# Cross-covariance attention on one core: Q and K of four units in rows of 8 KB

## The chip, the cores and the metric

The kernel runs on one core of a Trainium2 chip. The metric is the device time in microseconds. The kernel before takes 127.44 us, the median of three runs (127.34 to 127.64).

## The reference

For each of 8 x 12 = 96 heads, Q, K and V are 512 x 64 in f32. Q and K are normalised along the sequence, so each of the 64 columns is divided by its own norm; the attention is 64 x 64, column against column:

```python
Q_norm = Q / (np.linalg.norm(Q, axis=-2, keepdims=True) + 1e-10)
K_norm = K / (np.linalg.norm(K, axis=-2, keepdims=True) + 1e-10)
attn = np.einsum('bhnd,bhne->bhde', Q_norm, K_norm)
attn = np.exp(attn - np.max(attn, axis=-1, keepdims=True))
attn = attn / (np.sum(attn, axis=-1, keepdims=True) + 1e-10)
return np.einsum('bhnd,bhde->bhne', V, attn).astype(np.float32)
```

Three inputs of 12.6 MB are read once and one output of 12.6 MB is written.

## The kernel before

The 96 heads are 12 units (s) of 8 heads. Two units make a pair (w), and V is loaded by pairs, in two halves of 1 MB.

Loads. `load_qk` (L213 to L223) brings Q or K of one unit, 1 MB, into a tile of 128 partitions. A head has 32 partitions and each of them 16 consecutive sequence rows, which are 4 KB in a row in memory; the 8 heads of a unit are two groups (r) of four, so a partition holds two such rows, one for each group. Unit 0 comes in halves (FINE). `load_v` (L225) gives a V head 16 partitions with 32 sequence rows each, 8 KB in a row. There are 7 buffers for Q and K together (`NB['qk']`), 3 for V and 6 for outputs (`NB['so']`).

Work on a unit. `cast_qk` (L244) makes bf16 copies with the two groups interleaved. `square` (L249) squares them for the norms, Q and K into one tile. `grams` (L258 to L263) runs 64 matmuls: for each of 16 sequence rows and each head slot h, the 32 partitions of a slot, 128 columns of K (two heads) against 128 of Q; of the 128 x 128 result only the two 64 x 64 diagonal blocks are used. `sums` (L265) adds the squares over partitions with a 0/1 matrix (`hm`), `fold` (L272) adds up the rest on DVE, `norms` (L276) turns the sums over with a selecting matrix, `powers` (L280) takes the power -1/2 on ACT. `scale_k` (L286) multiplies the gram by K's norms, `logits` (L290) transposes it on PE, `scales_q` (L294) multiplies by Q's norms in two halves, `exps` and `normalise` (L300, L304) make the attention matrix `ab` in bf16.

Work on V and the output. `cast_v` (L316), `vtrans` (L321, transposes on PE), `vcopy` (L328), then `outs` (L334, 32 matmuls for a quarter of a unit), `ocopy` (L344, out of PSUM into an output tile) and `store` (L229), 1 MB for a unit. The store of unit 9 is cut into four (CUTS, one of them 124 partitions and one 4), and units 10 and 11 are stored in halves (HALF).

The order. All DMAs but two are issued by SP, in one queue. A planner (`Order`, L75) writes out one order for all engines before anything is built: each piece of work has engines with a cost, pieces that must be done first, and a rank (R, and QK_PACE, V_FROM, V_PACE, ST_LAG for DMAs); where several pieces can start at about the same time, the lowest rank goes first. A piece that may run on several engines (CHOICE) is put where cost plus BIAS ends first. Casts may be on DVE, ACT or POOL, squares on DVE or ACT, `vcopy` and `ocopy` on ACT or DVE. A DMA of 512 KB is costed at X = 1.27 us, and at most 8 are in flight. Each engine then runs its list in that order.

Of the kernel before, what the change touches and what calls it, by code (L numbers as in the profile page):

```python
# [18 lines left out]
 'R': {'ck': 14.3601,  # L19
       'q': -46.9145,  # L20
       'sq': -4.5261,
       'sk': 21.309,
       'gr': 31.9137,
       's1': -8.269,
       'rd': 14.1273,
       'nn': -13.565,
       'pw': -22.1669,
       'kx': 16.8281,
       'lg': -36.3133,
       'qs': 14.727,  # L30
       'ex': 7.4539,
       'nm': 23.5766,
       'cv': -5.1919,
       'vt': 13.5707,
       'vc': 31.4911,
       'ou': -17.6156,
       'oc': 6.4318},
 'BIAS': {('cv', 'DVE'): 12.3272,
          ('vc', 'ACT'): 5.2627,
          ('oc', 'DVE'): 7.9654,  # L40
          ('q0', 'ACT'): -9.0842,
          ('sk', 'ACT'): 4.174,
          ('sk', 'DVE'): 5.4091,
          ('cv', 'ACT'): 0.906,
          ('cv', 'POOL'): -0.1651,
          ('ck', 'DVE'): -11.8527,
          ('ck', 'ACT'): -10.4645,
          ('ck', 'POOL'): -15.4937,
          ('oc', 'ACT'): 4.7795,
          ('sq', 'DVE'): -12.3114,  # L50
          ('sq', 'ACT'): -21.9953,
          ('q0', 'DVE'): -28.6804,
          ('q0', 'POOL'): -29.3142,
          ('vc', 'DVE'): -20.4676},
 'QK_PACE': 0.9356,
 'V_FROM': 0.0874,
 'V_PACE': 0.7666,
 'ST_LAG': 6.0835,
 'SPLIT': 3,
 'HALF': (10, 11),  # L60
 'WAKE': ('SP',),
 'CUTS': ((0, 0, 6, 0, 124), (0, 0, 6, 124, 128), (0, 6, 16, 0, 128), (1, 0, 16, 0, 128))}
# [89 lines left out]
def kernel(  # L152
# [13 lines left out]
    FINE = PAR["FINE"]  # L166
# [13 lines left out]
    qmp = ctx.enter_context(tc.tile_pool(name="qmp", bufs=NB["qm"]))  # L180
    sqp = ctx.enter_context(tc.tile_pool(name="sqp", bufs=NB["sq"]))
# [59 lines left out]
    def heads(c):  # L241
        return slice(0, 2) if c is None else slice(c, c + 1)

    def cast_qk(eng, s, x, c):  # L244
        if (s, x) not in qkb:
            qkb[s, x] = qmp.tile([128, TT, 2, D], BF16, name="qb" if x == 0 else "kb")
        copy(eng, qkb[s, x][:, :, heads(c)], qk32[s, x][:, cols(c)].rearrange("p (r t) d -> p t r d", t=TT))

    def square(eng, s, x, c):  # L249
        if s not in sq:  # L250
            sq[s] = sqp.tile([128, 2, TT, 2, D], BF16, name="sq")
        o, i = sq[s][:, x, :, heads(c)], qkb[s, x][:, :, heads(c)]
        if eng == "ACT":
            nc.scalar.activation(o, i, AF.Square)  # L254
        else:
            nc.vector.tensor_tensor(out=o, in0=i, in1=i, op=ALU.mult)

    def grams(s):  # L258
        gram[s] = ps_g.tile([128, HU, 4, 2 * D], F32, name="gram")
        for t in range(TT):  # L260
            for h in range(HU):
                q, k = (qkb[s, x][32 * h:32 * (h + 1), t].rearrange("p r d -> p (r d)") for x in range(2))
                nc.tensor.matmul(gram[s][:, h, 0], k, q, start=(t == 0), stop=(t == TT - 1))  # L263

    def sums(s):  # L265
        st[s] = ps_l.tile([D, 4, 2 * D], F32, name="l")
        for t in range(0, TT, 4):
            for x in range(2):
                nc.tensor.matmul(st[s][32 * x:32 * (x + 1)].rearrange("p t d -> p (t d)"), hm,  # L269
                                 sq[s][:, x, t:t + 4].rearrange("p t r d -> p (t r d)"), start=(t == 0), stop=(t == TT - 4))  # L270

    def fold(s):  # L272
        s2[s] = small.tile([D, 2 * D], F32, name="s2")
        nc.vector.tensor_reduce(out=s2[s], in_=st[s].rearrange("p t d -> p d t"), axis=mybir.AxisListType.X, op=ALU.add)  # L274

    def norms(s):  # L276
        nn[s] = ps_l.tile([128, 2 * HU], F32, name="l")
        nc.tensor.matmul(nn[s], s2[s], sel, start=True, stop=True)  # L278

    def powers(s):  # L280
        ln = small.tile([128, 2 * HU], F32, name="ln")
        r12[s] = small.tile([128, 2 * HU], F32, name="r12")
# [3 lines left out]
    def scale_k(s):  # L286
        kqs[s] = small.tile([128, HU, 2 * D], F32, name="kqs")
        nc.vector.tensor_tensor(out=kqs[s], in0=gram[s][:, :, 0], in1=r12[s][:, HU:, None].to_broadcast([128, HU, 2 * D]), op=ALU.mult)  # L288

    def logits(s):  # L290
        for h in range(HU):
            nc.tensor.transpose(gram[s][:, h, 1], kqs[s][:, h], ident)  # L292

    def scales_q(s, r):  # L294
        if r == 0:
            ls[s] = small.tile([128, HU, D], F32, name="ls")
        half = (LO, HI)[r]
        nc.vector.tensor_tensor(out=ls[s][half], in0=gram[s][half, :, 1, half], in1=r12[s][half, :HU, None].to_broadcast([D, HU, D]), op=ALU.mult)  # L298
# [66 lines left out]
    hm = const.tile([128, 32], BF16, name="hm")  # L365
    nc.gpsimd.memset(hm, 0.0)
    own = const.tile([128, HU], F32, name="own")
    nc.vector.tensor_reduce(out=own, in_=ident.rearrange("p (h i) -> p h i", h=HU), axis=mybir.AxisListType.X, op=ALU.add)
    nc.vector.tensor_copy(hm[:, 0:HU], own)
    sel = const.tile([D, 2 * HU], F32, name="sel")  # L370
    for x in range(2):
        nc.gpsimd.tensor_copy(sel[:, HU * x:HU * (x + 1)], ident[0:D, 32 * x:32 * x + HU])
# [6 lines left out]
    def size(key):  # L379
        n = {"gr": 128, "s1": 16, "nn": 4, "lg": 8, "vt": 8, "ou": 32}[key[0]]  # L380
        return n // 2 if key[0] == "vt" and key[-1] is not None else n

    LOCK = {"ck", "q0", "sq", "sk", "nm", "cv"}
# [11 lines left out]
    CHOICE = ("ck", "q0", "sq", "sk", "cv", "vc", "oc")  # L395
# [17 lines left out]
    def uses(i):  # L413
        s, x = divmod(i, 2)
        return every("ck" if x else "q0", s)

    last = None
    for s in range(S):
        for c in parts(s):
            for x in range(2):  # L420
                key = ("l" + "qk"[x], s, c)
                piece(key, {"DMA": 2 * X if c is None else X}, uses(2 * s + x - NB["qk"]), [last],
                      PAR["QK_PACE"] * ((s + 0.5 * (c or 0)) / S), load_qk, s, x, c)
                last = key
    SM = NB["sm"]
    for s in range(S):
        for c in parts(s):
            dve, act, tt = two(c, 0.16, 0.52), two(c, 0.18, 0.84), two(c, 0.16, 0.52)
            for x, (load, cast, sqr, rank) in enumerate((("lq", "q0", "sq", "q"), ("lk", "ck", "sk", "ck"))):
                free = [("gr", s - NB["qm"])] + every(sqr, s - NB["qm"]) if s >= NB["qm"] else []  # L430
                piece((cast, s, c), {"DVE": dve, "ACT": act, "POOL": 2 * dve}, [(load, s, c)] + free, [], R[rank] + 0.01 * s, cast_qk, s, x, c)
                piece((sqr, s, c), {"DVE": tt, "ACT": act}, [(cast, s, c), back("s1", s, NB["sq"])], [], R[sqr] + 0.01 * s, square, s, x, c)
        piece(("gr", s), {"PE": 1.2}, every("ck", s) + every("q0", s) + [back("qs", s, 1, 0), back("qs", s, 1, 1)], [], R["gr"] + 0.01 * s, grams, s)
        piece(("s1", s), {"PE": 1.2}, every("sk", s) + every("sq", s) + [back("pw", s, 1)], [], R["s1"] + 0.01 * s, sums, s)
        piece(("rd", s), {"DVE": 0.69}, [("s1", s), back("nn", s, SM)], [], R["rd"] + 0.01 * s, fold, s)
        piece(("nn", s), {"PE": 0.3}, [("rd", s)], [], R["nn"] + 0.01 * s, norms, s)
        piece(("pw", s), {"ACT": 0.52}, [("nn", s), back("qs", s, SM, 0), back("qs", s, SM, 1)], [], R["pw"] + 0.01 * s, powers, s)
        piece(("kx", s), {"DVE": 0.69}, [("gr", s), ("pw", s), back("lg", s, SM)], [], R["kx"] + 0.01 * s, scale_k, s)
        piece(("lg", s), {"PE": 0.7}, [("kx", s)], [], R["lg"] + 0.01 * s, logits, s)
        for r in range(2):  # L440
            piece(("qs", s, r), {"DVE": 0.43}, [("lg", s), back("ex", s, SM)], [("qs", s, 0)] if r else [], R["qs"] + 0.01 * s, scales_q, s, r)
        piece(("ex", s), {"ACT": 0.425}, [("qs", s, 0), ("qs", s, 1), back("nm", s, SM)], [], R["ex"] + 0.01 * s, exps, s)
# [6 lines left out]
    for w in range(W):  # L449
# [9 lines left out]
        for n, (q, f) in enumerate(turns(w)):  # L459
# [3 lines left out]
            else:  # L463
                wait = [("qs", S - 1, 0), ("qs", S - 1, 1)] + ([("vc", w, *turns(w)[n - 4])] if n >= 4 and turns(w)[n - 4][1] is not None else [])
# [57 lines left out]
```

## Time and profile before

| what | value |
|---|---|
| median of 3 runs | 127.44 us (127.34 to 127.64) |
| the profiled execution | 127.3 us |
| its span, first to last instruction | 125.2 us |
| TensorE clock granted, mean | 0.875 |
| HBM read, written | 37.75 MB, 12.58 MB |
| instructions | 4066 |

The profile is of one execution. Its first part gives the busy time of each engine, its second cuts the span in 40 slices and shows the busy share of each in tenths, its third the DMA queues; q1 is SP's queue, q10 ACT's, q8 and q14 are instruction fetches and small loads. The chain follows the work that ended last back to the start. Groups of instructions are named by line and tiles; times of one instruction are in ns. The sixth part gives DMA issues by tile, with their size and the median time from issue to landing. PE is TensorE, DVE VectorE, ACT ScalarE, POOL GpSimd, SP SyncE.

### The profile page before, as it was taken

Reading aid. Unit: us, or ns where it says so; the run is one execution under the profiler, and the core shown is the slowest. Engines: PE = TensorE matmul, PEld = TensorE weight load, DVE = VectorE, ACT = ScalarE, POOL = GpSimd, SP = SyncE. Lnnn points to the kernel's source line nnn. Section 1 sums busy time; section 2 is a strip of 40 time slices with the busy share of each in tenths; the row PEclk is TensorE's granted clock in tenths of the full one; section 3 lists DMA queues with packets and bytes.
Section 4 is the critical chain, followed back from the end, with each engine's and each line's share of the span. In section 5 each row is a group of like instructions: output and inputs, shape, how many; then the busy total and the mean of one; then the engine's idle time right before and its main releaser. Section 6 shows DMA issues by size and latency. Waiting matters only on the chain.

```text
span 125.2 us, 4066 instructions
## 1 busy us (share of the span) xinstructions
PE 79.2 (63%) x1800; PEld 52.6 (42%) x1800; DVE 78.9 (63%) x140; ACT 84.9 (68%) x116; POOL 47.5 (38%) x40
## 2 busy tenths in 40 slices
PE   0019369873598787859637798882898879941000
PEld 0024254561474475538525455461275456630000
DVE  2043475876852989987987599993799978700000
ACT  4068594784698853998799997938958697863000
POOL 3330665382627088061806925065144810000000
PEclk9999955999657999995999999999599999997555
DMA  3999999999999999999999999999999999999993
GB/s 129 399 419 431 424 411 418 427 419 415 420 424 423 420 428 408 421 414 428 410 432 424 410 421 415 429 414 420 427 428 410 416 416 414 418 408 412 415 395 154
DMA packets 11785, 50.59 MB, mean 404 GB/s; under 512 B 888, under 2 KB 1016, under 8 KB 10232
## 3 DMA queue, kind: packets, MB, share of 16 engines
q1 hardware_dynamic: 11480, 49.29, 95.8%
q10 hardware_dynamic: 288, 1.05, 2.3%
q8 instruction: 14, 0.23, 0.7%
q14 instruction: 3, 0.02, 0.0%
HBM read 37.75 MB, written 12.58 MB: 402 GB/s over the span
## 4 chain that ended last, share of the span: by engine, by line
DMA 70%; PE 9%; ACT 5%; DVE 4%; issue 2%; SPq 1%; ACTq 0%
DMA qk<-in_Q_dram 37%; DMA out_dram<-so 17%; DMA qk<-in_K_dram 16%; ACT so L207 5%; PE po L341 3%; PE gram L263 2%; PE gram L292 1%; PE vps L326 1%; DVE kqs L288 1%; DVE qb L209 1%; PE l L269 1%; DVE ab L313 1%; DVE s L274 0%; PE l L278 0%; ACT ln L283 0%
## 5 line engine op out<-in xcount | busy, mean ns | idle before, releaser
L211 POOL TENSOR_SCALAR kb<-qk 128x2048 bf16<-128x2048 f32 (+1 forms) x13 | 23.0, 1771 | 37.8 <-DMA qk<-in_K_dram 30.9
L254 ACT ACTIVATE sq<-qb 128x2048 bf16<-128x2048 bf16 (+1 forms) x13 | 23.1, 1776 | 7.8 <-DVE qb L209 7.6
L207 ACT COPY so<-po 128x512 f32<-128x512 f32 x47 | 25.6, 584 | 3.9 <-PE po L341 2.3
L211 POOL TENSOR_SCALAR vb<-v 128x1024 bf16<-128x1024 f32 x15 | 21.4, 1444 | 13.4 <-DMA v<-in_V_dram 9.6
L341 PE MATMUL po<-ab,vt 128*32 128x128 bf16 x768 | 20.2, 232 | 6.6 <-ACT so L207 2.1
L263 PE MATMUL gram<-qb,kb 32*128 32x128 bf16 x768 | 15.5, 237 | 12.3 <-DVE qb L209 8.8
L209 DVE CAST qb<-qk 128x2048 bf16<-128x2048 f32 (+1 forms) x12 | 13.7, 1143 | 11.2 <-DMA qk<-in_Q_dram 10.7
L326 PE MATMUL vps<-ident,vb 128*128 128x128 f32 x96 | 17.3, 305 | 4.7 <-POOL vb L211 2.7
L269 PE MATMUL l<-sq,hm 128*32 128x512 bf16 x96 | 18.4, 442 | 1.7 <-ACT sq L254 1.6
L263 PEld LDWEIGHTS <-kb 32*128 32x128 bf16 x768 | 13.3, 104 | 14.4 <-POOL kb L211 10.3
L341 PEld LDWEIGHTS <-vt 128*32 128x32 bf16 x768 | 13.8, 101 | 12.4 <-issue 7.9
L209 DVE COPY vt<-vps 128x1024 bf16<-128x1024 bf16 (+1 forms) x25 | 16.5, 665 | 3.4 <-PE vps L326 3.1
L207 ACT CAST vb<-v 128x1024 bf16<-128x1024 f32 x9 | 12.1, 1341 | 8.8 <-DMA v<-in_V_dram 8.6
L254 ACT ACTIVATE sq<-kb 128x2048 bf16<-128x2048 bf16 (+1 forms) x10 | 17.3, 1733 | 0.6 <-POOL kb L211 0.6
L326 PEld LDWEIGHTS vps<-ident,vb 128*128 128x128 f32 x96 | 11.2, 151 | 8.5 <-POOL vb L211 3.2
L274 DVE TENSOR_REDUCE s<-l 64x128 f32<-64x512 f32 x12 | 8.1, 677 | 6.5 <-PE l L269 6.5
L298 DVE TENSOR_TENSOR ls<-gram,r 64x256 f32<-64x256 f32 x24 | 10.1, 420 | 2.2 <-PE gram L292 1.9
L292 PE MATMUL gram<-ident,kqs 128*128 128x128 f32 x48 | 9.0, 316 | 3.5 <-DVE kqs L288 3.0
L288 DVE TENSOR_TENSOR kqs<-gram,r 128x512 f32<-128x512 f32 x12 | 8.3, 689 | 3.7 <-ACT r L284 3.1
L313 DVE TENSOR_TENSOR ab<-ex,rb 128x512 bf16<-128x512 f32 x12 | 9.3, 773 | 0.4
L269 PEld LDWEIGHTS <-hm 128*32 128x32 bf16 x96 | 5.5, 104 | 9.4 <-issue 7.4
L292 PEld LDWEIGHTS gram<-ident,kqs 128*128 128x128 f32 x48 | 5.7, 154 | 7.4 <-DVE kqs L288 6.6
(25 smaller groups left out, 40.2 us busy)
## 6 DMA issues: line engine op xcount, KB each, us to landing
v<-in_V_dram SPq DMA_DIRECT2D x12, 1024.0 KB, 19.8
qk<-in_Q_dram SPq DMA_DIRECT2D x11, 1024.0 KB, 19.8
qk<-in_K_dram SPq DMA_DIRECT2D x11, 1024.0 KB, 19.6
out_dram<-so SPq DMA_DIRECT2D x9, 1024.0 KB, 19.7
out_dram<-so SPq DMA_DIRECT2D x5, 512.0 KB, 9.4
qk<-in_K_dram ACTq DMA_DIRECT2D x2, 512.0 KB, 4.6
qk<-in_Q_dram SPq DMA_DIRECT2D x2, 512.0 KB, 6.3
out_dram<-so SPq DMA_DIRECT2D x1, 320.0 KB, 10.1
```

The costliest lines, as they stand in the source:

```text
L207: nc.scalar.copy(o, i)
L209: nc.vector.tensor_copy(o, i)
L211: nc.gpsimd.tensor_scalar(out=o, in0=i, scalar1=1.0, scalar2=0.0, op0=ALU.mult, op1=ALU.add)
L254: nc.scalar.activation(o, i, AF.Square)
L263: nc.tensor.matmul(gram[s][:, h, 0], k, q, start=(t == 0), stop=(t == TT - 1))
L269: nc.tensor.matmul(st[s][32 * x:32 * (x + 1)].rearrange("p t d -> p (t d)"), hm, sq[s][:, x, t:t + 4].rearrange("p t r d -> p (t r d)"), s ...
L288: nc.vector.tensor_tensor(out=kqs[s], in0=gram[s][:, :, 0], in1=r12[s][:, HU:, None].to_broadcast([128, HU, 2 * D]), op=ALU.mult)
L292: nc.tensor.transpose(gram[s][:, h, 1], kqs[s][:, h], ident)
L298: nc.vector.tensor_tensor(out=ls[s][half], in0=gram[s][half, :, 1, half], in1=r12[s][half, :HU, None].to_broadcast([D, HU, D]), op=ALU.mult)
L313: nc.vector.tensor_tensor(out=ab[s], in0=ex[s][:, :, None, :].to_broadcast([128, HU, 2, D]), in1=rb[:, :, :, None].to_broadcast([128, HU, ...
L326: nc.tensor.transpose(ps[:, n], vb[w][:, j].rearrange("p r d c -> p (r d c)").bitcast(F32), ident)
L341: nc.tensor.matmul(po[s, x][32 * h:32 * (h + 1), j].rearrange("p r d -> p (r d)"), v, ab[s][:, h].rearrange("p r d -> p (r d)"), start=Tru ...
```

## The change

Q and K of units 1 to 4 (LONG) are loaded like V: a head has 16 partitions with 32 sequence rows each, 8 KB in a row. The two groups of heads then lie in the two halves of the partitions, and each half is a DMA of its own, of 64 partitions. Such a unit is worked on differently:

- 32 partitions, one slot of the matmuls, now hold two heads. Q is copied twice to bf16 (`mask_q`), once with the partitions of the odd head set to zero and once with those of the even one (`par` is a 0/1 column); K is copied once, without interleaving.
- The gram matmul takes K (128 columns: two sequence rows) against both masked copies of Q (256 columns).
- Q is squared from its f32 tile, on ACT only.
- The two sequence rows are added up after the gram: `logits` multiplies by `eye2`, two identities one above the other, in place of the transpose. `scale_k` runs in two halves, `scales_q` in one step.
- The norms have other selecting matrices (`hm`, `sel` with 12 columns), built at the start by a few more small instructions.

For all units the squares of Q and K have a tile each, and their sums are separate pieces, each with two row groups of PSUM (b = 32 * (2 * x + n % 2)). The ranks and biases of the planner are all new, so the order of all work and the engine of most casts and copies differ. POOL's cost for casts in the planner is 1.5 times DVE's in place of 2. Buffers keep their numbers; the bf16 copies of K get a pool of their own.

```diff
+ 'LONG': (1, 2, 3, 4),
+ 'XL': 1.2575,
...
+    Ql, Kl = (x.rearrange("b h (p t) d -> (b h p) (t d)", t=T).rearrange("(w r e p) x -> w e r p x", r=2, e=2, p=4 * T // 2) for x in (Q, K))
...
-        if c is None:
+        if s in LONG:
+            for r, half in enumerate((LO, HI)):
+                issue.dma_start(out=o[half], in_=(Ql, Kl)[x][w, e, r])
+        elif c is None:
...
+        if s in LONG:
+            qkb[s, x] = kbp.tile([128, T, D], BF16, name="kb")
+            copy(eng, qkb[s, x], qk32[s, x])
+            return
...
+    def mask_q(eng, s, r):
+        if (s, 0) not in qkb:
+            qkb[s, 0] = qmp.tile([128, 2, T, D], BF16, name="qb")
+        o, i, m = qkb[s, 0][:, r], qk32[s, 0], par[:, r:r + 1]
+        if eng == "ACT":
+            nc.scalar.activation(o, i, AF.Copy, scale=m)
+        else:
+            (nc.vector if eng == "DVE" else nc.gpsimd).tensor_scalar(out=o, in0=i, scalar1=m, scalar2=0.0, op0=ALU.mult, op1=ALU.add)
...
+                p = slice(32 * h, 32 * (h + 1))
+                if s in LONG:
+                    o = gram[s][:, h, 0:2]
+                    q, k = qkb[s, 0][p, :, 2 * t:2 * t + 2].rearrange("p r t d -> p r (t d)"), qkb[s, 1][p, 2 * t:2 * t + 2].rearrange("p t d -> p (t d)")
...
+            if s in LONG:
+                nc.tensor.matmul(gram[s][:, h, 2, LO], kqs[s][:, h], eye2, start=True, stop=True)
+            else:
+                nc.tensor.transpose(gram[s][:, h, 1], kqs[s][:, h], ident)
...
- 'QK_PACE': 0.9356,
- 'V_FROM': 0.0874,
- 'V_PACE': 0.7666,
- 'ST_LAG': 6.0835,
+ 'QK_PACE': 15.9432,
+ 'V_FROM': 1.2527,
+ 'V_PACE': 10.4878,
+ 'ST_LAG': 17.0031,
```

On SP's queue the loads now come in the order V, Q1, K1, V, Q2, K2, V and so on, where before Q1, K1, V, V, Q2, K2 began it. Two full stores are issued before the last V load, where one was.

More of the change, by code (lines that the diff above doesn't have):

```diff
@@ L18 @@
  'X': 1.27,
[L19 to L54, printed above, removed]
@@ L55 @@
- 'QK_PACE': 0.9356,
- 'V_FROM': 0.0874,
- 'V_PACE': 0.7666,
- 'ST_LAG': 6.0835,
+ 'R': {'ck': -22.4355,
+       'q': -58.979,
+       'sq': 8.8953,
+       'sk': 87.461,
+       'gr': 115.1078,
+       's1': 72.6482,
+       'rd': 61.2414,
+       'nn': -14.167,
+       'pw': -122.7448,
+       'kx': -4.8738,
+       'lg': -47.4763,
+       'qs': -27.9749,
+       'ex': 38.4008,
+       'nm': -4.3242,
+       'cv': -20.2888,
+       'vt': 86.5781,
+       'vc': -27.908,
+       'ou': 26.3559,
+       'oc': 86.0175},
@@ new lines @@
+ 'BIAS': {('cv', 'DVE'): 3.5472,
+          ('vc', 'ACT'): 33.8237,
+          ('oc', 'DVE'): 9.7574,
+          ('q0', 'ACT'): 8.6126,
+          ('sk', 'ACT'): -50.3485,
+          ('sk', 'DVE'): 76.2585,
+          ('cv', 'ACT'): 2.2132,
+          ('cv', 'POOL'): 3.0663,
+          ('ck', 'DVE'): 28.4022,
+          ('ck', 'ACT'): -2.9809,
+          ('ck', 'POOL'): -27.8906,
+          ('oc', 'ACT'): 9.3321,
+          ('sq', 'DVE'): 33.0171,
+          ('sq', 'ACT'): 32.675,
+          ('q0', 'DVE'): -43.3867,
+          ('q0', 'POOL'): -44.9347,
+          ('vc', 'DVE'): 6.6412,
+          ('q1', 'DVE'): -47.1557,
+          ('q1', 'ACT'): 31.7402,
+          ('q1', 'POOL'): -58.5001},
@@ L261, in grams @@
             for h in range(HU):
[L262 to L270, printed above, removed]
+                p = slice(32 * h, 32 * (h + 1))
@@ new lines, in grams, with sums @@
+                if s in LONG:
+                    o = gram[s][:, h, 0:2]
+                    q, k = qkb[s, 0][p, :, 2 * t:2 * t + 2].rearrange("p r t d -> p r (t d)"), qkb[s, 1][p, 2 * t:2 * t + 2].rearrange("p t d -> p (t d)")
+                else:
+                    o = gram[s][:, h, 0]
+                    q, k = (qkb[s, x][p, t].rearrange("p r d -> p (r d)") for x in range(2))
+                nc.tensor.matmul(o, k, q, start=(t == 0), stop=(t == TT - 1))
+    def sums(s, x):
+        if s not in st:
+            st[s] = ps_l.tile([128, 8 * D], F32, name="l")
+        m = hm[:, 1] if s in LONG else hm[:, 0]
+        for n in range(4):
+            b = 32 * (2 * x + n % 2)
+            nc.tensor.matmul(st[s][b:b + 32], m, sq[s, x][:, 4 * n:4 * n + 4].rearrange("p t r d -> p (t r d)"), start=(n < 2), stop=(n >= 2))
@@ L272, in fold @@
     def fold(s):
-        s2[s] = small.tile([D, 2 * D], F32, name="s2")
-        nc.vector.tensor_reduce(out=s2[s], in_=st[s].rearrange("p t d -> p d t"), axis=mybir.AxisListType.X, op=ALU.add)
+        d = D if s in LONG else 2 * D
+        s2[s] = small.tile([128, 2 * D], F32, name="s2")[:, 0:d]
+        nc.vector.tensor_reduce(out=s2[s], in_=st[s].rearrange("p (t d) -> p d t", d=d), axis=mybir.AxisListType.X, op=ALU.add)
     def norms(s):
-        nn[s] = ps_l.tile([128, 2 * HU], F32, name="l")
@@ L278, in norms @@
-        nc.tensor.matmul(nn[s], s2[s], sel, start=True, stop=True)
+        nn[s] = ps_l.tile([128, 12], F32, name="l")
+        if s in LONG:
+            for r, half in enumerate((LO, HI)):
+                nc.tensor.matmul(nn[s][half], s2[s], sel[:, 1 + r], start=True, stop=True)
+        else:
+            nc.tensor.matmul(nn[s], s2[s], sel[:, 0], start=True, stop=True)
     def powers(s):
-        ln = small.tile([128, 2 * HU], F32, name="ln")
-        r12[s] = small.tile([128, 2 * HU], F32, name="r12")
+        ln = small.tile([128, 12], F32, name="ln")
@@ L283, in powers, with scale_k @@
+        r12[s] = small.tile([128, 12], F32, name="r12")
         nc.scalar.activation(ln, nn[s], AF.Ln, bias=tiny[:, 0:1])
         nc.scalar.activation(r12[s], ln, AF.Exp, scale=-0.5)
-    def scale_k(s):
-        kqs[s] = small.tile([128, HU, 2 * D], F32, name="kqs")
-        nc.vector.tensor_tensor(out=kqs[s], in0=gram[s][:, :, 0], in1=r12[s][:, HU:, None].to_broadcast([128, HU, 2 * D]), op=ALU.mult)
+    def scale_k(s, n):
+        if n == 0:
+            kqs[s] = small.tile([128, HU, 2 * D], F32, name="kqs")
+        if s in LONG:
+            half = (LO, HI)[n]
+            nc.vector.tensor_tensor(
+                out=kqs[s][half].rearrange("p (g x) (r d) -> p r g x d", x=2, r=2), in0=gram[s][half, :, 0:2, half].rearrange("p (r g) x d -> p r g x d", r=2),
+                in1=r12[s][half, HU:].rearrange("p (r g x) -> p r g x", r=2, x=2)[:, :, :, :, None].to_broadcast([D, 2, 2, 2, D]), op=ALU.mult)
+        else:
+            nc.vector.tensor_tensor(out=kqs[s], in0=gram[s][:, :, 0], in1=r12[s][:, HU:2 * HU, None].to_broadcast([128, HU, 2 * D]), op=ALU.mult)
@@ L290, in logits @@
     def logits(s):
         for h in range(HU):
-            nc.tensor.transpose(gram[s][:, h, 1], kqs[s][:, h], ident)
+            if s in LONG:
+                nc.tensor.matmul(gram[s][:, h, 2, LO], kqs[s][:, h], eye2, start=True, stop=True)
+            else:
+                nc.tensor.transpose(gram[s][:, h, 1], kqs[s][:, h], ident)
     def scales_q(s, r):
@@ L296, in scales_q @@
             ls[s] = small.tile([128, HU, D], F32, name="ls")
+        if s in LONG:
+            nc.vector.tensor_tensor(out=ls[s], in0=gram[s][:, :, 2, LO], in1=r12[s][:, :HU, None].to_broadcast([128, HU, D]), op=ALU.mult)
+            return
         half = (LO, HI)[r]
@@ L414, in uses @@
         s, x = divmod(i, 2)
-        return every("ck" if x else "q0", s)
+        return every("ck", s) if x else every("q0", s) + (every("q1", s) + every("sq", s) if s in LONG else [])
     last = None
@@ L421 @@
                 key = ("l" + "qk"[x], s, c)
-                piece(key, {"DMA": 2 * X if c is None else X}, uses(2 * s + x - NB["qk"]), [last],
+                piece(key, {"DMA": (2 if c is None else 1) * (PAR["XL"] if s in LONG else X)}, uses(2 * s + x - NB["qk"]), [last],
                       PAR["QK_PACE"] * ((s + 0.5 * (c or 0)) / S), load_qk, s, x, c)
@@ L439 @@
-        piece(("lg", s), {"PE": 0.7}, [("kx", s)], [], R["lg"] + 0.01 * s, logits, s)
-        for r in range(2):
+                long = s in LONG and x == 0
+                fn = (mask_q, s, 0) if long else (cast_qk, s, x, c)
+                piece((cast, s, c), {"DVE": dve, "ACT": act, "POOL": 1.5 * dve}, [(load, s, c)] + free, [], R[rank] + 0.01 * s, *fn)
+                if long:
+                    piece(("q1", s, c), {"DVE": dve, "ACT": act, "POOL": 1.5 * dve}, [(load, s, c)] + free, [], R[rank] + 0.01 * s, mask_q, s, 1)
@@ new lines @@
+                piece((sqr, s, c), {"ACT": act} if long else {"DVE": tt, "ACT": act}, [(load if long else cast, s, c), back("s1", s, 1, x)], [],
+                      R[sqr] + 0.01 * s, square, s, x, c)
+        lng = s in LONG
+        scaled = lambda n: [back("qs", s, n, r) for r in range(1 if s - n in LONG else 2)]
+        piece(("gr", s), {"PE": 1.9 if lng else 1.2}, every("ck", s) + every("q0", s) + (every("q1", s) if lng else []) + scaled(1), [],
+              R["gr"] + 0.01 * s, grams, s)
@@ new lines @@
+        for x in range(2):
+            piece(("s1", s, x), {"PE": 0.6}, every("sk" if x else "sq", s) + [back("pw", s, 1)], [], R["s1"] + 0.01 * s, sums, s, x)
+        piece(("rd", s), {"DVE": 0.69}, [("s1", s, 0), ("s1", s, 1), back("nn", s, SM)], [], R["rd"] + 0.01 * s, fold, s)
+        piece(("nn", s), {"PE": 0.3}, [("rd", s)], [], R["nn"] + 0.01 * s, norms, s)
+        piece(("pw", s), {"ACT": 0.52}, [("nn", s)] + scaled(SM), [], R["pw"] + 0.01 * s, powers, s)
+        for n in range(2 if lng else 1):
+            piece(("kx", s, n), {"DVE": 0.69}, [("gr", s), ("pw", s), back("lg", s, SM)], [("kx", s, 0)] if n else [], R["kx"] + 0.01 * s, scale_k, s, n)
@@ L441 @@
+        piece(("lg", s), {"PE": 1.5 if lng else 0.7}, [("kx", s, n) for n in range(2 if lng else 1)], [], R["lg"] + 0.01 * s, logits, s)
+        for r in range(1 if lng else 2):
             piece(("qs", s, r), {"DVE": 0.43}, [("lg", s), back("ex", s, SM)], [("qs", s, 0)] if r else [], R["qs"] + 0.01 * s, scales_q, s, r)
-        piece(("ex", s), {"ACT": 0.425}, [("qs", s, 0), ("qs", s, 1), back("nm", s, SM)], [], R["ex"] + 0.01 * s, exps, s)
+        piece(("ex", s), {"ACT": 0.425}, scaled(0) + [back("nm", s, SM)], [], R["ex"] + 0.01 * s, exps, s)
@@ L463 @@
             else:
-                wait = [("qs", S - 1, 0), ("qs", S - 1, 1)] + ([("vc", w, *turns(w)[n - 4])] if n >= 4 and turns(w)[n - 4][1] is not None else [])
+                wait = [("qs", S - 1, r) for r in range(1 if S - 1 in LONG else 2)] + ([("vc", w, *turns(w)[n - 4])] if n >= 4 and turns(w)[n - 4][1] is not None else [])
             piece(("vt", w, q, f), {"PE": 0.5 if f is not None else 0.68}, [("cv", w, r, c) for r in range(2) for c in range(2)] + wait, [turned],
```

55 lines of the change are left out of this document (33 added, 22 removed).

## The prediction

> **What bounds the kernel now.** I read the page from the top: busy shares, then the slices, then the queues, then the chain. No compute engine is busy for more than 68% of the span. The DMA engines are busy in every slice except the first and the last:
>
> ```profile
> PE 79.2 (63%) x1800; PEld 52.6 (42%) x1800; DVE 78.9 (63%) x140; ACT 84.9 (68%) x116; POOL 47.5 (38%) x40
> ...
> DMA  3999999999999999999999999999999999999993
> GB/s 129 399 419 431 424 411 418 427 419 415 420 424 423 420 428 408 421 414 428 410 432 424 410 421 415 429 414 420 427 428 410 416 416 414 418 408 412 415 395 154
> DMA packets 11785, 50.59 MB, mean 404 GB/s; under 512 B 888, under 2 KB 1016, under 8 KB 10232
> ## 3 DMA queue, kind: packets, MB, share of 16 engines
> q1 hardware_dynamic: 11480, 49.29, 95.8%
> ...
> DMA 70%; PE 9%; ACT 5%; DVE 4%; issue 2%; SPq 1%; ACTq 0%
> ```
>
> The reader is to see the unbroken row of nines and a rate that stays between 399 and 432 GB/s while loads and then stores run. The bytes are fixed by the task: 37.7 MB in, 12.6 MB out. So the end is the sum of packet times on 16 engines, and an edit can move it in two ways: it changes the time of packets, or it lets the engines run dry. The issues say how far the queue is ahead:
>
> ```profile
> v<-in_V_dram SPq DMA_DIRECT2D x12, 1024.0 KB, 19.8
> qk<-in_Q_dram SPq DMA_DIRECT2D x11, 1024.0 KB, 19.8
> qk<-in_K_dram SPq DMA_DIRECT2D x11, 1024.0 KB, 19.6
> out_dram<-so SPq DMA_DIRECT2D x9, 1024.0 KB, 19.7
> ```
>
> A transfer lands 19.8 us after its issue, eight transfers of about 2.5 us. In the program's order each DMA waits for the eighth before it, so eight are always queued. A late compute engine costs nothing until it is later than this queue is long.
>
> **What a row costs.** The trace has a record for each packet, and a row is one packet. The DMA answers for two stretches, one with nearly only 4 KB rows (26 to 32 us) and one with mostly the 8 KB rows of V (15 to 17.4 us), give the time of each:
>
> ```profile
> DMA packets 640, 2.50 MB, mean 416 GB/s; under 512 B 33, under 2 KB 33, under 8 KB 639
> ## 3 DMA queue, kind: packets, MB, share of 16 engines
> q1 hardware_dynamic: 639, 2.48, 101.2%
> ```
>
> ```profile
> DMA packets 147, 1.00 MB, mean 418 GB/s; under 512 B 16, under 2 KB 16, under 8 KB 33
> ## 3 DMA queue, kind: packets, MB, share of 16 engines
> q1 hardware_dynamic: 147, 1.00, 99.1%
> ```
>
> First: 1.012 x 6000 ns x 16 = 97.2 us in 606 packets of 4 KB and 33 completions of 9 ns: 160 ns each. Second: 0.991 x 2400 x 16 = 38.1 us, less 17 packets of 4 KB, in 114 of 8 KB: 309 ns. Packet by packet it is sharper: 8,686 of the 8,832 4 KB records of the main queue last 159 ns, 1,534 of the 1,536 8 KB ones 309 ns. Two short rows therefore record 318 ns against 309. Records overlap a little (shares above 100%), so the pace is less: the commonest distance between starts is 155.3 ns (310.7 for two) in stretches of 4 KB and 306 ns in stretches of 8 KB.
>
> **The change, part by part.**
>
> *8 KB rows.* Q and K of units 1 to 4 are 8 loads of 1 MB; 2,048 packets of 4 KB become 1,024 of 8 KB. By the pace this saves 1,024 x 4.7 ns / 16 = 0.30 us; by the record lengths 1,024 x 9 / 16 = 0.58 us. Each load becomes two DMAs of 64 partitions, so 8 more DMAs, each with 16 completions of 9 ns, one per engine: 0.07 us more. Bounds 0 (the pace a long row has when it is not V's) to 0.58; I take the pace, because it is what adds up to the end: 0.30 - 0.07 = **0.23 us less**.
>
> *More DMAs in the queue.* Eight lanes now hold a mix of 0.5 and 1 MB: five DMAs carry Q, K and V, 3 MB, so eight carry 4.8 MB, 12 us instead of 19.8, while the long loads run. A buffer that comes free late eats these 12 us first. K of unit 3 takes the buffer of Q of unit 0, which is cast by about 10 us; 10 MB stand before it, so the engines reach it near 28. Q of unit 5 takes that of K of unit 1: landed near 15.5, cast by 19 (behind two masked copies), reached after 15 MB, near 40. So nothing runs dry; cost 0. Without that cover the cost is the delay itself.
>
> *Masked Q.* POOL gets 8 masked copies and 18 full casts of Q and K (12 now), 4 halves (2 now), and gives away 10 of its 15 V casts; DVE loses all casts of Q. No masked copy is in this trace; the same form, a tensor-scalar over 128x2048 from f32 to bf16, takes 1,903 ns on POOL. Below that there is no reason; above, the farthest row of that size is 1,909 on ACT. POOL has 26 such, 4 halves at 1,048, 5 V casts at 1,444 and 2 us of constants: 63 us against 47.5. In a long unit it has 3 x 1.9 = 5.7 us of work per 7.5 us of loads (Q, K, V). Covered.
>
> *ACT.* 22 squares of 1,908, 3 halves of 1,040, 15 V casts of 1,341, 31 copies out of 584 and 12 x 0.89 of small ones make 94 us; the same sum for the kernel before gives 91 where the page has 84.9 busy (neighbours overlap). So about 88. *DVE* loses 10 casts of 1,225 and 3 squares and gains 16 copies out of 673, 4 V casts (0.7, from the nearest copies) and small constants: about 80.
>
> *PE.* The grams of four units have 256 columns per matmul instead of 128. 64 matmuls take 1.07 to 1.90 us now, so at most 1.9 us more per unit, below nothing excluded: 4 to 8 us. The logits become 4 matmuls of 64 columns, norms 2 instead of 1 (0.4 us per pair of passes): 1 to 3 us. PE ends below 90 of 125 us.
>
> *The order and the tail.* Every transfer, cast and store moves, but the sums above leave each compute engine 35 us idle. The tail needs a look of its own: behind the last V load stand 10 MB of stores instead of 11 (two stores now go before it, one before). Now that load lands at 97.4 us (the POOL cast that waited for it starts at 97.44), and the last copy out ends at
>
> ```profile
> 111.99 1.68 ACT L207 COPY so<-po 128x512 f32<-128x512 f32 x3 [0.95 <-PE po L341]
> ```
>
> 113.7 us, 16.3 us later, while engines go on to about 123. With one store less behind it, the load lands 2.5 - 0.2 us later, at 99.7; the last copy is at 116.0; the last half store (1.3 us of packets) must be queued some 2 us ahead, by 119.3. 3 us of cover remain; before it was 5.5. Cost 0, and 1 us for each us beyond 3.
>
> **Sum.** The profiled execution took 127.3 us (span 125.2): 127.3 - 0.23 = **127.1 us**. The median of the runs is 127.44, 0.1 above it; from there the sum is 127.2. A measurement of this kernel can tell about 0.2% (0.25 us) from no change, so the forecast lies on that edge.
>
> **Rivals.**
>
> *The half tile is slow* (slower). All loads of before write 128 partitions with 16 engines. A long load writes 64, all 16 engines in the same half. If two engines that write the same half share one way into SBUF, each packet takes up to twice 309 ns: 1,024 x 309 / 16 = 19.8 us more, **147 us**. It decides early: 4.7 ns, 1.5% of a packet, eats the whole saving, and a stretch of 10% gives 129. For it: no row shows such a load. Against it: one store in the trace is cut into 124 and 4 partitions. The queue has 840 four-byte completions for 54 DMAs, which is 52 x 16 + 2 x 4, so those two ran on 4 engines, with 31 rows each from all over the tile, while the other 12 went on with the next store's 2,560 B rows from the same partitions. All 128 packets of 1,536 B took 65 ns, starting 61 ns apart, and all 128 of 2,560 B took 102. Nothing stretched; but stores read SBUF, and loads write it. The Trainium skill speaks against the change here: SBUF — State Buffer, section "Door 1: The DMA port swizzle", says that partitions 0 to 63 reach 8 of 16 ports and measured 196 GB/s at 1 MiB against 328 for 128; DMA: Bandwidth & Descriptors, "Rules for kernel authors", says that transfers to the two halves serialize. By 196 GB/s, an estimate, 8.4 MB would take 43 us instead of 20 and the sum would be 150. The 65 ns rows do not bear it out for reads; no run shows writes. I give 15% to the full or nearly full stretch, 7% to one of up to 10%.
>
> *The saving does not show* (no change, 127.2 to 127.7). The 0.23 us sit on all engines alike, but the last one ends the run, and in the last 3 us the engines finish one by one (in the DMA answer for 114 to 126 us the digits fall from 9 by 8 and 6 to 4). The trace has 14 instruction packets of 0.94 us; one that falls on another engine hides 0.23 us either way. For it: the size of the saving; against it: PE, with by far the most instructions, keeps its 3,315 rows in the order. 33%.
>
> *Compute becomes late* (slower). ACT has the most work, and the tail cover falls to 3 us. If the chain from the last V to the last copy grew from 16.3 to 21 us, the end would move by 1.7 us, to 128.8. For it: 16 copies out move to DVE; against it: the idle sums. 3%.
>
> *The long rows do not happen* cannot be: the program's order shows 16 loads of 64x2048.
>
> **Numbers.** The forecast with the upper part of its bounds (126.7 to 127.19 us, 0.2% under the median): faster 42%. Same 33%. Slower 15 + 7 + 3 = 25%. The likeliest case's own range is 126.7 to 127.5; with the small stretch and a late tail the range is 126.7 to 129.0, and 147 is left out with its 15%.
>
> **What would show it.** Right: nines in all inner slices, about 10,900 packets, 8 KB records of 309 ns for Q and K of units 1 to 4 as for V, POOL near 63 us. Wrong: long-row records above 314 ns, GB/s below 400 between 10 and 40 us (the half tile); a digit below 9 after 100 us, or SP waiting for ACT or DVE at the last stores (late compute); masked copies above 2.5 us, with which POOL no longer keeps pace with 2.5 us per load.

## The result, and the profile after

The changed kernel takes 148.91 us, the median of six runs (147.89 to 149.84), against 127.39 for the kernel before beside it: 1.168 times as long, with an interval of 1.162 to 1.174. The profiled execution took 149.24 us with a span of 147.3, 22.1 us more than before. Single runs of a kernel lie 1 to 5% apart where the transfers of four units are split by halves or in three, and in the experiment with the order alone; in the others they lie within 0.6%, but for one run named below.

These are the lines of the changed kernel's page that answer to those shown of before:

```profile
span 147.3 us, 4163 instructions
...
PE 87.9 (60%) x1824; PEld 59.1 (40%) x1824; DVE 78.8 (54%) x152; ACT 89.1 (60%) x108; POOL 64.1 (44%) x51
...
DMA  5999999999999999999999999999999999999980
GB/s 176 417 386 220 218 354 218 231 276 271 216 231 298 216 222 295 375 420 419 418 426 426 417 410 418 423 420 435 407 419 420 425 409 417 416 416 402 396 339 17
DMA packets 10890, 50.60 MB, mean 343 GB/s; under 512 B 1016, under 2 KB 1144, under 8 KB 8312
## 3 DMA queue, kind: packets, MB, share of 16 engines
q1 hardware_dynamic: 10584, 49.29, 95.1%
...
DMA 61%; PE 19%; ACT 5%; DVE 4%; issue 3%; POOL 1%; SPq 1%; POOLq 0%
```

The row of nines is unbroken, as before: the DMA engines do not lack work until the last two slices. But the rate below it is not. From the fourth slice to the sixteenth, about 10 to 59 us, it falls to 216 to 231 GB/s, with humps where a V load comes between; from about 63 us it stays near 400 and more almost to the end. A busy share of 9 with half the rate means that the packets got longer. The low stretch is just the one in which the long loads run.

How much longer is seen in the DMA answer for 10 to 18.5 us, in which nearly all packets are long rows of Q and K:

```profile
DMA packets 281, 1.90 MB, mean 224 GB/s; under 512 B 49, under 2 KB 49, under 8 KB 49
## 3 DMA queue, kind: packets, MB, share of 16 engines
q1 hardware_dynamic: 281, 1.90, 103.1%
```

1.031 x 8500 ns x 16 engines = 140.2 us in 232 packets of 8 KB and 49 small ones: about 600 ns a row, where V's rows took 309. Over the whole run the records of the data packets sum to 143.4 us per engine (all of them over 16) against 123.4 before. That is 20.0 of the 22.1 us. The other 2.1 show at the very end, here in the answer for 142 to 147 us:

```profile
DMA  9999766644310000000000000000000000000000
GB/s 393 393 426 426 295 262 262 262 164 164 131 66 33 33 33 33 0 33 33 33 33 33 0 33 33 33 33 0 33 33 33 33 0 0 0 0 0 0 0 0
```

Each of the 40 columns is 125 ns, and 33 GB/s is one packet of 4 KB in it. From about 143.7 us to the last packet's end at 146.2 one packet follows another, so the last 2.5 us are a single engine that fell behind the other 15.

### The profile page after: what moved, and what is told of

Same layout as the page of the kernel before. It is cut to its first block, busy times and chain, and to the rows that moved or that the text cites. A ratio compares the mean times of both kernels' runs of the same rounds, so it can differ in the third digit from the quotient of the medians.

```text
span 147.3 us, 4163 instructions
## 1 busy us (share of the span) xinstructions
PE 87.9 (60%) x1824; PEld 59.1 (40%) x1824; DVE 78.8 (54%) x152; ACT 89.1 (60%) x108; POOL 64.1 (44%) x51
## 2 busy tenths in 40 slices
DMA packets 10890, 50.60 MB, mean 343 GB/s; under 512 B 1016, under 2 KB 1144, under 8 KB 8312
## 4 chain that ended last, share of the span: by engine, by line
DMA 61%; PE 19%; ACT 5%; DVE 4%; issue 3%; POOL 1%; SPq 1%; POOLq 0%
DMA v<-in_V_dram 30%; DMA qk<-in_Q_dram 17%; DMA out_dram<-so 14%; PE po L397 6%; PE vps L382 4%; PE gram L300 4%; PE gram L343 2%; PE l L308 2%; ACT sq L285 2%; ACT so L216 2%; POOL qb L220 1%; PE gram L345 1%; DVE kqs L334 1%; ACT vb L216 1%; DVE vt L218 1%
## 5 line engine op out<-in xcount | busy, mean ns | idle before, releaser
L216 ACT CAST vb<-v 128x1024 bf16<-128x1024 f32 x15 | 20.1, 1357 | 19.5 <-DMA v<-in_V_dram 19.4
L300 PE MATMUL gram<-qb,kb 32*128 32x128 bf16 (+1 forms) x768 | 21.5, 272 | 16.6 <-POOL kb L220 16.1
L308 PE MATMUL l<-sq,hm 128*32 128x512 bf16 x96 | 17.0, 459 | 17.8 <-ACT sq L285 10.7
L275 POOL TENSOR_SCALAR qb<-qk,par 128x2048 bf16<-128x2048 f32 x8 | 15.7, 1976 | 24.4 <-DMA qk<-in_Q_dram 24.4
L220 POOL TENSOR_SCALAR qb<-qk 128x2048 bf16<-128x2048 f32 (+1 forms) x9 | 16.3, 1814 | 16.3 <-PE gram L300 9.0
L218 DVE COPY vt<-vps 128x1024 bf16<-128x1024 bf16 (+1 forms) x25 | 16.7, 666 | 5.3 <-PE vps L382 5.1
L216 ACT COPY so<-po 128x512 f32<-128x512 f32 x31 | 17.1, 580 | 4.0 <-PE po L397 2.7
L218 DVE COPY so<-po 128x512 f32<-128x512 f32 x17 | 11.6, 688 | 8.1 <-PE po L397 6.3
L313 DVE TENSOR_REDUCE s<-l 128x128 f32<-128x512 f32 (+1 forms) x12 | 8.2, 687 | 13.5 <-PE l L308 13.5
L285 ACT ACTIVATE sq<-qb 128x2048 bf16<-128x2048 bf16 (+1 forms) x8 | 14.4, 1800 | 1.4 <-POOL qb L220 1.2
L308 PEld LDWEIGHTS <-hm 128*32 128x32 bf16 x96 | 4.1, 100 | 19.9 <-issue 19.6
L285 ACT ACTIVATE sq<-qk 128x2048 bf16<-128x2048 f32 x4 | 7.6, 1906 | 5.7 <-DMA qk<-in_Q_dram 5.7
L220 POOL TENSOR_SCALAR vb<-v 128x1024 bf16<-128x1024 f32 x5 | 7.5, 1493 | 7.9 <-DMA v<-in_V_dram 6.7
```

The costliest lines, as they stand in the source:

```text
L216: nc.scalar.copy(o, i)
L218: nc.vector.tensor_copy(o, i)
L220: nc.gpsimd.tensor_scalar(out=o, in0=i, scalar1=1.0, scalar2=0.0, op0=ALU.mult, op1=ALU.add)
L275: (nc.vector if eng == "DVE" else nc.gpsimd).tensor_scalar(out=o, in0=i, scalar1=m, scalar2=0.0, op0=ALU.mult, op1=ALU.add)
L300: nc.tensor.matmul(o, k, q, start=(t == 0), stop=(t == TT - 1))
L308: nc.tensor.matmul(st[s][b:b + 32], m, sq[s, x][:, 4 * n:4 * n + 4].rearrange("p t r d -> p (t r d)"), start=(n < 2), stop=(n >= 2))
```

## The experiments

**Theories.** (H) A DMA whose 64 partitions are all in one half of the tile is slow, because its 16 engines share what leads into that half, two and two. (O) The other order of all work, or the masked work, starves the transfers. (R) 8 KB rows of Q and K are slow as such. (D) A DMA of 64 partitions, or more DMAs, are slow wherever they write.

### The order alone

The changed kernel without long units:

```diff
- 'LONG': (1, 2, 3, 4),
+ 'LONG': (),
```

> The changed kernel with no unit in LONG: the new ranks and placement of all work, none of the long loads, masked copies or wide grams (the planner orders what is left by the same ranks). If the loads to half of the partitions are what is slow, this is 127.4 us, within 0.5 of before, with 4 KB records of 159 ns throughout. If the other order of all work starves the transfers, most of the 21 us stay, 140 us or more, and slices below 9 appear in the DMA row.

Its times do not agree with each other: 127.07 us once, 130.29 with the profile, and 133.5 to 133.7 four times. No median of it is compared. In its page the loads run at full rate, and the loss is at the other end:

```profile
DMA  3999999999999999999999999999999999796991
GB/s 150 390 428 411 432 411 431 413 416 431 412 422 426 413 421 417 423 417 414 418 422 428 421 414 428 418 414 426 427 407 421 418 418 408 312 376 205 413 411 66
```

Here the engines do run dry (7, 9, 6 near 110 to 118 us), since the stores come late. It is an order of its own, because the planner made it for other work; it shows what late compute looks like, and that the low rate of 10 to 59 us goes with the long loads.

### The halves alone, in the kernel before

```diff
-        if c is None:
+        if s in (1, 2, 3, 4):
+            for part in (slice(0, 64), slice(64, 128)):
+                issue.dma_start(out=o.rearrange("p (r x) -> p r x", r=2)[part], in_=i[part])
+        elif c is None:
```

> The kernel before, with each of the 8 loads of Q and K of units 1 to 4 split into two DMAs of 64 partitions (0 to 63 and 64 to 127); rows stay 4 KB, order and compute stay. If it is the half of the partitions, the 2,048 short packets take twice 159 ns: 2,048 x 159 / 16 = 20.4 us more, 147 to 149 us, and 218 GB/s while they run. If it is the 8 KB row, the extra work or the new order, it stays at 127.4 to 127.7.

147.85 us, 1.161 times before (1.155 to 1.166). Nothing is different from before but eight loads cut in two, rows, order and computation included, and the page shows the same stretch at half rate:

```profile
DMA  5999999999999999999999999999999999999991
GB/s 190 395 248 214 278 423 238 211 265 291 223 216 228 213 244 386 424 436 406 420 421 412 425 432 406 419 415 430 411 430 423 418 410 409 424 407 415 415 387 79
```

The data packets sum to 143.1 us per engine, 19.6 more than before (20.4 were forecast). This split alone costs 20.5 us, nearly all of the 21.5 that the change cost, so O and R are out as its causes; H and D are left.

### Even and odd partitions

The same split, with the parts `slice(0, 128, 2)` and `slice(1, 128, 2)`:

> The same split of the same 8 loads of the kernel before, by even and odd partitions: 64 partitions for each DMA, as many DMAs and bytes as in the split by halves, but each spreads over the whole tile. If the engines are slow because two of them write into the same half, this costs only 8 more DMAs: 127.3 to 127.8 us, records of 159 ns. If any DMA of 64 partitions (512 KB) is slow, or only half of the engines work on it, 147 to 149 us as with the halves.

128.22 us, 1.0065 times before (1.005 to 1.008). So 64 partitions and 512 KB are not slow by themselves: D is out. The split costs 0.8 us where at most 0.4 was forecast. The table by stretches shows one place, 8 to 10 us (columns: stretch, its length, busy us and instructions of PE, PEld, DVE, ACT and POOL, granted clock, DMA share, GB/s). First the even and odd split, then the kernel before:

```profile
8.00:10.00 2.00, 1.22 (x48) 1.31 (x52) 0.73 (x1) 2.00 (x3) 0.18 (x1) 1.00 0.89 299
```

```profile
8.00:10.00 2.00, 1.22 (x48) 1.32 (x52) 0.73 (x1) 2.00 (x3) 0.18 (x1) 1.00 1.03 424
```

125 GB/s less for 2 us is 0.6 us of full rate. It happens at the first split load and not at the later seven. The queue is not empty there: the 4 KB records that start from 8 to 9 us last 243 ns on the mean, against 159 before and after. Why these stretch stays open.

Then the changed kernel with its long loads so placed, and nothing else edited. The heads lie where masks and selecting matrices do not expect them, so units 1 to 4 compute other values:

```diff
-            for r, half in enumerate((LO, HI)):
-                issue.dma_start(out=o[half], in_=(Ql, Kl)[x][w, e, r])
+            for r in range(2):
+                issue.dma_start(out=o[r::2], in_=(Ql, Kl)[x][w, e, r])
```

> The changed kernel with one edit: the two DMAs of a long load write even and odd partitions instead of the lower and the upper half. The heads then lie on other partitions than masks and selecting matrices take them to, so the values of units 1 to 4 are other ones; every instruction and every byte stays. If it is the half, everything comes back and the saving of the long rows shows: 127.0 to 127.4 us, 8 KB records of 309 ns. If it is the length of the row, the masked work, or 64 partitions as such, it stays at 147 to 150.

127.14 us, 0.998 times before (0.997 to 0.999). All 21.5 us came back with the destination of 16 DMAs. The sources in memory, the row length, the count of DMAs, the order and every instruction are those of the changed kernel. The same 8.5 us as above:

```profile
DMA packets 540, 3.65 MB, mean 430 GB/s; under 512 B 94, under 2 KB 94, under 8 KB 94
## 3 DMA queue, kind: packets, MB, share of 16 engines
q1 hardware_dynamic: 540, 3.65, 102.0%
```

1.020 x 8500 x 16 = 138.7 us in 446 rows and 94 small packets: 309 ns a row, and 430 GB/s for 224.

### The middle of the tile

The kernel before, each of the eight loads in three parts: 32 to 95, 0 to 31, 96 to 127.

> The kernel before, with each of the 8 loads of Q and K of units 1 to 4 split into three DMAs: partitions 32 to 95, 0 to 31 and 96 to 127; rows 4 KB. If two engines are in each other's way only where both write the same half of the tile, the middle DMA, which has its first rows in the lower half and its last in the upper, runs at full pace (159 ns a record), and only the two outer ones, 1,024 packets, at half: 1,024 x 159 / 16 = 10.2 us more, 137 to 139 us. If any load to an unbroken range of fewer than 128 partitions is slow, all 2,048 packets are: 147 to 149.

139.55 us in the profiled execution and 142.9 in the other one; 137 to 139 was forecast. The data packets sum to 134.8 us per engine, 11.4 more than before (10.2 forecast, and 20 if an unbroken range were enough). The three parts can be told apart where such a load follows one of V, as Q of unit 2 does: its first 128 rows are the part 32 to 95, the rest the two outer ones. First the answer for 19.4 to 20.6 us, then that for 20.8 to 22.4:

```profile
DMA packets 130, 0.49 MB, mean 410 GB/s; under 512 B 12, under 2 KB 12, under 8 KB 128
## 3 DMA queue, kind: packets, MB, share of 16 engines
q1 hardware_dynamic: 130, 0.49, 99.8%
```

```profile
DMA packets 131, 0.43 MB, mean 271 GB/s; under 512 B 25, under 2 KB 25, under 8 KB 131
## 3 DMA queue, kind: packets, MB, share of 16 engines
q1 hardware_dynamic: 131, 0.43, 106.8%
```

In the first all 116 rows of 4 KB last 159 ns; in the second 106 rows last 255 ns on the mean. So 64 partitions in a row run at full pace where they reach into both halves, and 32 partitions within one half do not. Counted in the order of the queue, middle parts that follow on outer ones last 191 to 233 ns on the mean; that engines are then out of step would explain it, but is not shown. So H stands. Its border between partition 63 and 64 fits all runs, and none of them places it more closely than between 32 and 95.

### One unit, and two queues

The split by halves for unit 1 only (`s == 1`):

> The kernel before with only unit 1's two loads split by halves: a quarter of the packets. If the price is that of packets in a row of busy engines, it is a quarter of 20 us: 512 x 159 / 16 = 5.1 us more, 132.4 to 132.8. If a part of it is hidden behind other waits, or is a late state that builds up, it is far from a quarter.

132.44 us, 1.040 times before (1.038 to 1.042): 5.0 us, a quarter of 20. The price is paid by the packet and nothing hides it.

The split by halves for four units, with the lower half issued by SP and the upper by ACT:

> The kernel before with the loads of units 1 to 4 split by halves, the lower half issued by SP and the upper by ACT, so that each engine finds both halves in two queues. If the engines go through the halves in step whatever the queue, it stays near 147. If having both at hand lets one engine of a pair take the upper half while the other takes the lower, the records fall towards 159 ns and the time towards 128 (more where ACT waits for its turn to issue).

147.84 us in the profiled execution and 151.19 in the other one, no better than the 146.96 and 148.75 of one queue. But its page has another shape:

```profile
DMA  4999999999999999999999999999999953477991
GB/s 164 393 278 347 360 284 301 310 295 375 355 225 274 391 423 420 420 418 428 411 423 428 414 416 425 415 421 424 419 418 416 419 207 155 199 292 244 387 411 61
...
q1 hardware_dynamic: 10456, 45.09, 81.1%
q10 hardware_dynamic: 1440, 5.24, 11.2%
```

The rate in the load stretch rises to 280 to 375 GB/s in most slices, and the data packets sum to 135.2 us, 11.8 over before instead of 19.6. With both halves at hand the engines seem to get out of each other's way for some of the time. What is gained goes again: between 117 and 128 us the share falls to 5, 3 and 4, since the stores come late; by the profile SP waits 16.7 us, before it can issue one of them, for a copy of ACT's into its output tile. ACT, which now also issues loads, was not looked into further.

### Reading by halves

The kernel before with the stores of units 1 to 4 split, 4 MB in 1,024 packets, loads untouched:

```diff
+        elif s in (1, 2, 3, 4):
+            for half in (LO, HI):
+                nc.sync.dma_start(out=Of[s // 2, s % 2][half], in_=so[s][half].rearrange("p r j d -> p r (j d)"))
```

> The kernel before with the stores of units 1 to 4 split into two DMAs of 64 partitions (lower and upper half), loads as they were. If only writing into SBUF shares a way (the 65 ns rows of the cut store said that reading does not), only 4 more DMAs are paid: 127.4 to 127.8 us, records of 159 ns. If reading shares it as well, the 1,024 packets of these stores take twice as long: 1,024 x 159 / 16 = 10.2 us more, 137 to 139.

131.69 us, the median of three runs, 1.032 times before (1.028 to 1.036); a fourth took 133.69. That is about 4 us (4.5 with the fourth run): neither of the two. In the stretch with these stores, 96 to 106 us, the engines go on almost as ever:

```profile
DMA packets 1101, 4.08 MB, mean 408 GB/s; under 512 B 117, under 2 KB 117, under 8 KB 1093
```

The 4 KB records of SP's queue have a mean of 161.1 ns (160.1 before), and the data packets sum to 0.7 us more per engine, where doubled packets would be 10.2. Yet the last packet ends at 127.1 us instead of 124.0; the engines finish over some 5 us instead of 3, and the last copy out of PSUM ends 3 us later. So that split was tried by even and odd partitions:

> The kernel before with the stores of units 1 to 4 split by even and odd partitions. The split of the stores by halves cost 4.5 us with hardly a stretched record. If that is what more DMAs in the queue of eight cost at the end of the run, this costs as much, 131 to 133 us. If it is the half after all, in a way that the records do not show, it goes: 127.4 to 127.9.

127.71 us, 1.0022 times before (1.0013 to 1.0031). Hence it is the half here as well, not the 4 more DMAs. Reading by halves does not double the packets as writing does; how its 4 us come about, when the records hardly stretch, stays open.

### The row alone, and a version that keeps it

The kernel before with the eight loads as whole DMAs of 128 partitions in 8 KB rows. It takes eight heads in a row, so these units compute with other heads' rows:

> The kernel before, with the 8 loads of Q and K of units 1 to 4 as one DMA each of 128 partitions with 8 KB rows (eight heads in a row, as V has them; these units therefore compute with the rows of other heads). No more DMAs than before, 1,024 packets of 8 KB for 2,048 of 4 KB. By the pace of the packets (4.7 ns saved a row) 0.30 us less than before, 127.06; by the record lengths 0.58 less, 126.8; nothing if the row length does not matter.

127.16 us, 0.9979 times before (0.9969 to 0.9989): 0.27 us less. One of its twelve runs took 129.13 and is not in the ratio. The pace of the packets (0.30) sized it, the record lengths (0.58) did not.

The changed kernel with even and odd partitions, and the rest made to fit: `par` marks even and odd partitions, `head` the pairs of slot and parity, and `scale_k` reads the gram straight.

```diff
-                out=kqs[s][half].rearrange("p (g x) (r d) -> p r g x d", x=2, r=2), in0=gram[s][half, :, 0:2, half].rearrange("p (r g) x d -> p r g x d", r=2),
+                out=kqs[s][half].rearrange("p h (r d) -> p h r d", r=2), in0=gram[s][half, :, 0:2, half],
...
+    nc.vector.tensor_reduce(out=head.rearrange("p (r h) -> p r h", r=2), in_=ident.rearrange("p (h i r) -> p r h i", h=HU, r=2), axis=mybir.AxisListType.X, op=ALU.add)
...
-    nc.vector.tensor_reduce(out=par, in_=ident.rearrange("p (h r i) -> p r h i", h=HU, r=2), axis=mybir.AxisListType.XY, op=ALU.add)
+    nc.vector.tensor_reduce(out=par, in_=ident.rearrange("p (i r) -> p r i", r=2), axis=mybir.AxisListType.X, op=ALU.add)
```

> The changed kernel with the long loads in even and odd partitions, and with masks, selecting matrices and the scaling by K's norms made for that layout (a slot of 32 partitions then holds head h of both groups, one in its even and one in its odd partitions). Same instructions but for the shape of a few small ones. By the shared half: 127.0 to 127.3, as with the loads alone moved, 0.1 to 0.3 us under before. If something else of the long units were slow beside the loads it would show here again.

127.13 us, 0.9973 times before (0.9963 to 0.9982). It computes what the reference does, and is 0.3 us faster than the kernel before and 21.8 faster than the changed one:

```profile
DMA  3999999999999999999999999999999999999993
GB/s 123 403 429 424 434 424 429 416 416 424 416 424 419 420 434 404 416 432 415 421 409 420 420 423 413 423 429 417 412 420 423 409 421 413 417 411 412 417 390 136
DMA packets 10890, 50.60 MB, mean 404 GB/s; under 512 B 1016, under 2 KB 1144, under 8 KB 8312
```

The packets are the same 10,890 as in the changed kernel; only their destination differs. With units 5 and 6 long as well:

> The version with long loads in even and odd partitions, with six long units instead of four (1 to 6). By the packets the step from four to six saves 4 x 512 rows' worth, 512 x 4.7 ns / 16 = 0.15 us, less 4 more DMAs' completions (0.04): 0.1 us under the version with four, 127.0. The planner makes another order for it and POOL and ACT get two more units of masked work: if that makes the last stores late, 128 or more.

127.05 us, 0.997 times before (0.996 to 0.998). The step from four to six is of the forecast's size, but within the intervals of the two.

## Why the prediction was wrong

**The step that failed** is the time of a packet of a long load. The sum took V's 309 ns for it and put the half of the tile at nothing, which gave 0.23 us less. In the changed kernel these packets last about 600 ns where they run alone, and the records sum to 20.0 us more per engine; written to even and odd partitions, the same packets are back at 309 ns.

The term was known: it stood as the rival "The half tile is slow", and its price (19.8 us, 147 us) and its sign in the profile (GB/s below 400 between 10 and 40 us, records above 314 ns) are what came. That 19.8 met 20.0 so closely is in part luck. Counted in the order of the queue, the 1,024 long rows last 588 ns on the mean, which is 17.8 us more, and rows of V between them are longer too, up to 418 ns on the mean of one load, which is about 2.5 more.

What was wrong is its weight. It got 15%, because the 65 ns records of the cut store were taken as evidence against it, with the remark that stores read and loads write. That remark was the point. The runs show both sides: loads by halves nearly double their packets, stores by halves leave them at 161 ns. Besides, by the prediction's own account those rows came from all over the tile and not from one half. The row was no row of the disputed operation, and it should have left the bounds, 0 and 19.8 us, as far apart as they were.

The Trainium skill's rule (SBUF — State Buffer, "Door 1: The DMA port swizzle") is borne out for writes: 219 to 224 GB/s in halves against 430 spread over the tile. It is borne out in the detail as well: a range across partition 64 ran at full pace where it ran alone. What its figure of 196 GB/s gave, 150 us, lies above the measured 148.9, and the row's bound, 147, below it. The traces do not name the engine of a packet nor its way into SBUF. So the runs show what a half costs and what avoids it; that two engines share one way is the rival's reason, which fits and is not shown.

**The saving of the 8 KB row** was right in kind and size, once its loads spread over the tile: 0.23 us was forecast for the change as made, and the changed kernel with spread loads gains 0.2 to 0.3 (127.14 and 127.13 against 127.36 and 127.45). Its bounds were right too; the pace between starts sized it, and the lengths of records, which overlap, say twice as much.

**More DMAs in the queue** cost nothing in the order of the changed kernel: the long loads in even and odd partitions have as many. In the order of the kernel before, the same split cost 0.8 us.

**Masked Q, ACT, DVE and PE** came as worked out: POOL 64.1 us (63), ACT 89.1 (88), DVE 78.8 (80), PE 87.9 (below 90). A masked copy takes 1,976 ns on POOL, against 1,903 for the row it was taken from:

```profile
L275 POOL TENSOR_SCALAR qb<-qk,par 128x2048 bf16<-128x2048 f32 x8 | 15.7, 1976 | 24.4 <-DMA qk<-in_Q_dram 24.4
```

Its 24.4 us of idle time end with loads of Q: POOL waits for the transfers, not they for it.

**The tail** held in this order: with even and odd partitions the last slices are those of before. The rival of late compute is real, though: it is what the order without long units shows.

**The range** (126.7 to 129.0) followed from the chances. With 15% it left the rival out; with a weight that the cut store had not lowered, it would have reached 147 at least. The page of the Trainium skill, which measured a transfer of partitions 0 to 63, deserved more weight than that row.

## What to carry to other kernels

When a kernel is bound by its transfers, look at the rate under the nines: full busy shares with half the rate are longer packets, and the place to look is where they are written. Where a load must be cut in two, cut it so that each part still spreads over the whole tile, as even and odd partitions do; in halves of the tile a row took 1.9 times as long. And a row that shows the opposite direction of a transfer is no evidence for this one.

## What the runs showed of the hardware that was not expected

Loads into one half of the partitions ran at 219 to 224 GB/s, and into every second partition at 430, with the same rows and the same number of DMAs. A load of partitions 32 to 95 kept 159 ns a row where it ran alone. Two queues that hold both halves brought most of the stretch to 280 to 375 GB/s. Stores out of one half kept 408 GB/s and 161 ns records, and yet the kernel ended about 4 us later. One engine alone carried the last 2.5 us of the changed kernel.
